# One-hot matrices of two tokens instead of four, built on a time budget, in a two-block transformer on one core

## The chip, the cores and the metric

The kernel runs on one NeuronCore of a Trainium2 chip. Its engines work side by side and wait for each other through semaphores: TensorE (PE, matmuls; PEld, its weight loads), VectorE (DVE), ScalarE (ACT), GpSimd (POOL) and SyncE (SP). Here SP only issues DMA transfers, and GpSimd only issues indirect ones. The metric is the device time of one execution in microseconds.

## What is computed

A sequence of 256 tokens with 1024 features passes two layers of a first block (four kinds of attention, then a gated MLP with a convolution) and two layers of a second block (a mixer, then a large mixture of experts). The change lies in the experts, `peer_ffn`. Each token has 8 heads, each head chooses 16 of 128 x 128 experts by the sum of two scores, and a softmax over the chosen scores gives the gates:

```python
    best_s, best_p = lax.top_k(cand_s, PEER_TOPK)
    idx = jnp.take_along_axis(cand_i, best_p, axis=-1)
    gate = jax.nn.softmax(best_s, axis=-1)
...
        act = jnp.einsum('td,thkd->thk', xb.astype(jnp.float32), u_tab[ib].astype(jnp.float32))
        wgt = jax.nn.gelu(act) * gb
        return jnp.einsum('thk,thkd->td', wgt, v_tab[ib].astype(jnp.float32))
```

## The kernel before

The kernel gathers no experts. In `peer` it multiplies all tokens with all 16384 rows of `u` (called U below), applies the gelu to the result, multiplies it with a dense table of gates that is zero where a token has not chosen an expert, and multiplies that with all of `v` (V). An expert has a number i * 128 + j; on chip i is the partition and j a column.

**Weights.** `weights` streams each matrix in units of 128 x 1024 fp32 (512 KB): SP issues the load into `wx` (3 buffers), ScalarE copies it to `wh` (4 buffers) with fewer mantissa bits, and VectorE writes the rest to `wl` (4 buffers, line 121). `mm3` then makes three matmuls for each product, with the high and low parts of the activations (`xh`, `xl`). U has 128 units in a layer, and so has V. `u_step` uses two units and fills two columns j of `at0` (j 0 to 63) or `at1` (j 64 to 127); 32 steps make a half of U.

**Gates.** The ranking (`select`) yields its work bit by bit, and `weave` puts it between the steps of U's first half: after each step, `beside` lets it have so many nanoseconds of VectorE by nominal costs, in the place behind the last `wl`. The gates of the two halves of the tokens then go two ways.
- The first 128 tokens: `scatter_gates` writes them into a zeroed table in HBM (`gates`) with 128 indirect DMAs of GpSimd (line 209), one for each head and rank. The 16 of a head wait until those of the head before have landed. `load_gates` (line 223) reads the table back on SP's queue, two columns j at a time, once the last head has landed; VectorE multiplies them into `at` (`v_split`), and `split` makes the high and low parts `eh` and `el` for V.
- The last 128 tokens: `build` makes the table's columns in PSUM. For four tokens it compares `io` with the chosen i and j (`oi`, `oj`), multiplies `oj` with three bf16 parts of the gates (`og`), and adds 12 matmuls of 128 x 128. VectorE multiplies the result into `at0` and into what `at1` holds so far; ScalarE copies the rest into `at1`, where later steps of U are multiplied in. One such group follows each step of U's second half.

**V.** `v_step` takes a pair of columns j (two units, 24 matmuls of 512 columns into the four banks `big`) and calls `v_split` for the next pair. The first pair is split by `first_split`, behind U.

The order of each engine's instructions is fixed when the program is built. The framework takes them from the code's order, lets an instruction go ahead of others where its own estimate of times says that it is ready, and inserts the semaphores. Each engine works its list in order, SP too.

Of the kernel before, what the change touches and what calls it, by code (L numbers as in the profile page):

```python
# [12 lines left out]
BF16 = mybir.dt.bfloat16  # L13
# [3 lines left out]
AF = mybir.ActivationFunctionType  # L17
OP = mybir.AluOpType
AX = mybir.AxisListType

T = 256
# [32 lines left out]
EARLY = 1  # L54
WARM = 10
LAG, TAIL, AHEAD, HOLD = 4, 2, 2, (2, 6)
SIDE_Q, SIDE_S = 2500, 2800
UQ_SIZES = [768, 512]
S2_SIZES = [1024] * 26

# [1 line left out]
class Net:  # L62
# [156 lines left out]

    def load_gates(self, l, n, pool):  # L220

        g = self.t(pool, [128, 2, 128], tag="gate", bufs=3)
        d = self.nc.sync.dma_start(g, self.gates[l][:, 2 * n:2 * n + 2]).ins
        for b in self.landed:
            self.tc.add_manual_dep(d, b.name, SYNC, reason="the gates have landed")
        return g
# [809 lines left out]
    def peer(self, l):  # L1036
# [3 lines left out]
        with ExitStack() as ctx:  # L1040
            ip = ctx.enter_context(self.pool("pi"))
            idx = self.t(ip, [128, 128], U32, tag="idx")
            gs = [self.t(ip, [128, 8, 16], tag=f"gs{tt}") for tt in range(2)]
            iT, jT = (self.t(ip, [128, 128], BF16, tag=n) for n in ("iT", "jT"))
            gT = self.t(ip, [128, 3, 128], BF16, tag="gT")
            io = self.t(ip, [128, 128, 4], BF16, tag="io")
            for _ in self.clear:
                pass
            self.clear = self.clear_gates(l + 1, 4) if l < DEPTH - 1 else iter(())
# [4 lines left out]
            def half_acts():  # L1054
                return self.t(ctx.enter_context(self.pool("pa")), [128, 64, T], tag="at")

            def u_step(at, jp, tb=0):

                ps = self.pj([128, 2, T])
                for m in range(2):  # L1060
                    self.proj_fm(w, ps[:, m])
                a = at[:, 2 * jp:2 * jp + 2]
                self.act(a[:, :, :T - tb], ps[:, :, :T - tb], AF.Gelu_apprx_tanh)
                if tb:
                    y = self.t(self.op, [128, 2, 128], tag="y", bufs=2)[:, :, :tb]
                    self.act(y, ps[:, :, T - tb:], AF.Gelu_apprx_tanh)
                    self.tt(a[:, :, T - tb:], a[:, :, T - tb:], y, OP.mult)

            def build(g):


                t0, done = 124 - 4 * g, 2 * g + 2
                oi, oj = (self.t(self.op, [128, 128, 4], BF16, tag=n, bufs=2) for n in ("oi", "oj"))
                og = self.t(self.op, [128, 3, 128, 4], BF16, tag="og", bufs=2)
                self.tt(oi, io, iT[:, None, t0:t0 + 4].to_broadcast([128, 128, 4]), OP.is_equal)
                self.tt(oj, io, jT[:, None, t0:t0 + 4].to_broadcast([128, 128, 4]), OP.is_equal)
                self.tt(og, oj[:, None].to_broadcast([128, 3, 128, 4]),
                        gT[:, :, None, t0:t0 + 4].to_broadcast([128, 3, 128, 4]), OP.mult)
                yield 1900
                ps = self.ps([128, 4, 128])  # L1080
                for k in range(4):
                    for n in range(3):
                        self.mm(ps[:, k], oi[:, :, k], og[:, n, :, k], k == 0 and n == 0, n == 2)
                ps = ps.rearrange("p t j -> p j t")
                t0 += 128
                a0, a1 = at0[:, :, t0:t0 + 4], at1[:, :, t0:t0 + 4]
                self.tt(a0, a0, ps[:, :64], OP.mult)
                self.tt(a1[:, :done], a1[:, :done], ps[:, 64:64 + done], OP.mult)
                if done < 64:
                    self.copy(a1[:, done:], ps[:, 64 + done:])  # L1090
                yield 700

            parts, loaded = {}, {}

            def g_load(n):
                if n < 64:
                    loaded[n] = self.load_gates(l, n, early)

            def v_split(n, pool):

                if n < 64:
                    g_load(n + 2)
                    a = (at0, at1)[n // 32][:, 2 * (n % 32):2 * (n % 32) + 2]
                    self.tt(a[:, :, :128], a[:, :, :128], loaded.pop(n), OP.mult)
                    h, low = (self.t(pool, [128, 2, T], F32R, tag=x, bufs=1 + (n > 0)) for x in ("eh", "el"))
                    self.split(h, low, a)
                    parts[n] = [(h[:, m], low[:, m]) for m in range(2)]

            def first_split():
                for n in range(2):  # L1110
                    g_load(n)
                v_split(0, early)

            def v_step(at, jp, half):
                units = [(next(w), x) for x in parts.pop(32 * half + jp)]
                last = half == 1 and jp == 31
                for u in [units] if last else [units[:1], units[1:]]:
                    self.out_tokens(u, half == 0 and jp == 0 and u[0] is units[0], last, end if last else None)
                    if u[0] is units[0]:
                        v_split(32 * half + jp + 1, vp)  # L1120
# [6 lines left out]
            def weave(step, side, per_step, then=None):  # L1127

                side = chain(side, (f() or 0 for f in [then] if f))
                left = 0.0  # L1130
                for jp in range(32):
                    step(jp)
                    left = self.beside(side, left + per_step)
                for _ in side:
                    pass
# [4 lines left out]
            with self.pool("pn") as npool:  # L1140
                lead = self.enter(npool, "add", self.v("n2"), w, self.t(npool, [128, 8, T], tag="xnew"))
                self.dump(f"xc{l}", self.xT)
                if l < DEPTH - 1:
                    nc.sync.dma_start(keep, self.xT)
                self.hctx.close()
                self.xctx.close()
                self.open_xs()
                pool = sctx.enter_context(self.pool("pk", "right"))
                self.token_column()
                if l == DEPTH - 1:  # L1150
                    nc.sync.dma_start(keep, self.rows_of(npool))
                it = self.t(pool, [128, 128], tag="iota")
                nc.sync.dma_start(it, self.a["iota"])
                io16 = self.t(pool, [128, 16, 128], BF16, tag="io16")
                rank = self.select(l, pool, w, lead, self.normed(npool, self.v("n2")), io16, gs, idx, (iT, jT, gT))
                self.copy(io16, it[:, 0:16, None].to_broadcast([128, 16, 128]))
                self.copy(io, it[:, :, None].to_broadcast([128, 128, 4]))
            self.xs = self.xh, self.xl
            at0 = half_acts()
            weave(lambda jp: u_step(at0, jp), rank, SIDE_S)  # L1160
            sctx.close()
            at1 = half_acts()
            with self.pool("po") as self.op:
                for g in range(32):
                    u_step(at1, g, 4 * g)
                    for _ in build(g):
                        pass
            early = ctx.enter_context(self.pool("pf"))
            first_split()
            self.hctx.close()  # L1170
            self.open_xt()
            if l < DEPTH - 1:
# [5 lines left out]
                end = to_output  # L1178
            vctx = ExitStack()
            vp = vctx.enter_context(self.pool("pv", "right"))  # L1180
            for half, at in enumerate((at0, at1)):
                weave(lambda jp: v_step(at, jp, half), iter(()), 0)
            vctx.close()
# [3 lines left out]
    def select(self, l, pool, w, lead, normed, io16, gs, idx, turned):  # L1187
# [63 lines left out]
        def rest_of_ranks():  # L1251
            yield from normed
            pend.sort(key=lambda x: x[0])
            for tt in range(2):
# [5 lines left out]
                for r in range(8):  # L1260
                    n = 16 if r == 0 else 8
                    o = 0 if r == 0 else 8 + 8 * r
# [5 lines left out]
                    yield 760  # L1268

                bt = best[tt]  # L1270
                g = gs[tt]
                self.tt(g, bt, bt[:, :, 0:1].to_broadcast([128, 8, 16]), OP.subtract)
                self.act(g, g, AF.Exp)
                s = self.t(pool, [128, 8], tag="s", bufs=2)
# [6 lines left out]
                pf = self.t(pool, [128, 128], tag="pf", bufs=2)  # L1281
# [19 lines left out]
                for c in range(2):  # L1301
                    f, e = (self.t(pool, [128, 16, 8, 16], BF16, tag=n) for n in ("fe", "e"))
                    self.copy(f, fa[:, :, c].rearrange("p h r -> p r h")[:, :, :, None].to_broadcast([128, 16, 8, 16]))
                    e, f = (x.rearrange("p r h k -> p r (h k)") for x in (e, f))
# [14 lines left out]
                iT, jT, gT = turned  # L1319
                ps = self.ps([128, 3, 128])  # L1320
# [8 lines left out]
                self.tt(gT[:, 2], rest, gT[:, 1], OP.subtract)  # L1329

        return rest_of_ranks()

    def run(self, parts=("f0", "f1", "s0", "s1")):
# [204 lines left out]
```

## Time and profile before

| | us |
|---|---|
| median of 3 runs | 2612.99 (2612.26 to 2613.42) |
| profiled execution | 2614.9 |
| its span | 2613.0 |
| TensorE busy | 2560.8 (98%) |
| VectorE busy | 1835.9 (70%) |
| ScalarE busy | 1383.7 (53%) |
| GpSimd busy | 463.4 (18%) |

The span runs from the first instruction to the last in the profiled execution; 1.9 us of the execution's time lie around it. Busy times of different engines overlap. The mean TensorE clock granted was 0.996 of full speed.

### The profile page before, as it was taken

To read this page: it belongs to the slowest core of one execution; us is meant where nothing else is said; L and a number is where in the kernel's file an instruction comes from. 1 tells how busy PE (TensorE), PEld (TensorE's weight loads), DVE (VectorE), ACT (ScalarE), POOL (GpSimd) and SP (SyncE) were. 2 spreads that over 40 slices of the span, in tenths; PEclk is the share of its full clock that TensorE was granted. 3 is DMA by queue.
4 is the path that set the end of the run, shared out by engine and by line. 5 is a ranking of instruction groups with operands and counts; after the bars stand their busy time and mean duration, and the time that the engine had idled before them with its cause. 6 is when DMAs were issued, how large, how long until landed. Compare 5 with 4: busy or idle time off the path is not lost.

```text
span 2613.0 us, 46153 instructions
## 1 busy us (share of the span) xinstructions
PE 2560.8 (98%) x18042; PEld 2366.2 (91%) x18042; DVE 1835.9 (70%) x3511; ACT 1383.7 (53%) x2128; POOL 463.4 (18%) x261
## 2 busy tenths in 40 slices
PE   8999999999999999999999999999999999999999
PEld 7799997999999999999878888999999999878887
DVE  6688777877887995666665555877994666675555
ACT  6565566655676554444444444776554443344443
POOL 0000000000000077773000000000178772000000
PEclk9999999999999999999999999999999999999999
DMA  8756652566535576665576666635576665676664
GB/s 281 235 179 192 183 174 79 153 192 183 175 116 185 170 185 186 149 150 149 193 249 203 194 194 193 185 107 187 173 191 179 148 150 148 212 248 194 194 194 158
DMA packets 195098, 470.95 MB, mean 180 GB/s; under 512 B 54644, under 2 KB 89588, under 8 KB 193856
## 3 DMA queue, kind: packets, MB, share of 16 engines
q1 hardware_dynamic: 158016, 467.86, 56.9%
q0 software_dynamic: 36864, 0.15, 3.6%
q8 instruction: 141, 2.31, 0.3%
q14 instruction: 77, 0.63, 0.1%
HBM read 447.86 MB, written 20.05 MB: 179 GB/s over the span
## 4 chain that ended last, share of the span: by engine, by line
PE 85%; DMA 6%; DVE 6%; ACT 2%; issue 1%; SPq 0%; ACTq 0%; DVEq 0%
PE pj L132 46%; PE big L132 31%; PE ps L132 7%; DMA gate<-gates 4%; DVE wl L121 2%; DMA wx<-in_w 1%; ACT wh L118 1%; PE ps L573 1%; DVE el L121 1%; DVE xn L124 0%; DVE at L121 0%; DVE xT L121 0%; DMA wx<-in_wq 0%; DVE xl L124 0%; DVE c L124 0%
## 5 line engine op out<-in xcount | busy, mean ns | idle before, releaser
L118 ACT ACTIVATE wh<-wx 128x1024 fp32r<-128x1024 f32 (+1 forms) x800 | 844.4, 1057 | 898.7 <-PE pj L132 356.1
L121 DVE TENSOR_TENSOR wl<-wx,wh 128x1024 fp32r<-128x1024 f32 (+1 forms) x800 | 975.0, 1220 | 453.8 <-ACT wh L118 446.4
L132 PE MATMUL pj<-xh,wh 128*128 128x256 f32 x3136 | 897.3, 286 | 10.5 <-ACT wh L118 7.9
L132 PE MATMUL pj<-xl,wh 128*128 128x256 f32 x3136 | 889.6, 284 | 3.3 <-DVE xl L124 2.7
L132 PE MATMUL pj<-xh,wl 128*128 128x256 f32 x3136 | 889.1, 284 | 3.8 <-DVE wl L121 3.8
L209 POOL DMA_INDIRECT gates<-gs,idx x256 | 462.9, 1808 | 1712.6 <-DVE idx L129 1591.8
L132 PEld LDWEIGHTS pj<-xh,wh 128*128 128x128 f32 x3136 | 601.2, 192 | 12.8 <-ACT wh L118 8.3
L132 PEld LDWEIGHTS pj<-xl,wh 128*128 128x128 f32 x3136 | 600.5, 191 | 7.9 <-DVE xl L124 6.5
L132 PEld LDWEIGHTS pj<-xh,wl 128*128 128x128 f32 x3136 | 599.9, 191 | 6.6 <-DVE wl L121 5.7
L132 PE MATMUL big<-wh,el 128*128 128x512 f32 x1024 | 402.1, 393 | 10.4 <-DVE el L121 10.3
L132 PE MATMUL big<-wh,eh 128*128 128x512 f32 x1024 | 400.0, 391 | 11.6 <-ACT eh L118 11.6
L132 PE MATMUL big<-wl,eh 128*128 128x512 f32 x1024 | 399.9, 390 | 0.0
L132 PEld LDWEIGHTS big<-wh,el 128*128 128x128 f32 x1024 | 193.1, 189 | 58.4 <-DVE el L121 19.2
L132 PEld LDWEIGHTS big<-wh,eh 128*128 128x128 f32 x1024 | 193.0, 189 | 52.6 <-ACT eh L118 12.2
L132 PEld LDWEIGHTS big<-wl,eh 128*128 128x128 f32 x1024 | 193.1, 189 | 39.6
L121 DVE TENSOR_TENSOR at<-at,ps 128x256 f32<-128x256 f32 (+20 forms) x128 | 45.1, 352 | 131.6 <-PE ps L132 131.6
L132 PE MATMUL ps<-og,oi 128*128 128x128 bf16 x768 | 101.5, 297 | 0.0
L132 PE MATMUL big<-gh,wh 128*128 128x256 f32 x352 | 99.1, 282 | 0.0
L132 PE MATMUL big<-gl,wh 128*128 128x256 f32 x352 | 98.9, 281 | 0.0
L132 PE MATMUL big<-gh,wl 128*128 128x256 f32 x352 | 98.8, 281 | 0.0
L121 DVE TENSOR_TENSOR at<-at,gate 128x256 f32<-128x256 f32 x128 | 52.9, 422 | 58.4 <-DMA gate<-gates 58.0
L121 DVE TENSOR_TENSOR el<-at,eh 128x512 fp32r<-128x512 f32 x128 | 87.2, 684 | 0.0
(355 smaller groups left out, 3309.0 us busy)
## 6 DMA issues: line engine op xcount, KB each, us to landing
wx<-in_u SPq DMA_DIRECT2D x256, 512.0 KB
wx<-in_v SPq DMA_DIRECT2D x256, 512.0 KB
wx<-in_wm SPq DMA_DIRECT2D x132, 512.0 KB
wx<-in_w SPq DMA_DIRECT2D x88, 512.0 KB
gates<-zero SPq DMA_DIRECT2D x128, 128.0 KB
wx<-in_wo SPq DMA_DIRECT2D x32, 512.0 KB
wx<-in_wq SPq DMA_DIRECT2D x32, 512.0 KB
gate<-gates SPq DMA_DIRECT2D x128, 128.0 KB
```

Source lines behind the costliest of these rows:

```text
L118: return self.nc.scalar.activation(out, in_, AF.Copy)
L121: return self.nc.vector.tensor_tensor(out, a, b, op=op)
L132: return self.nc.tensor.matmul(ps, w, x, start=start, stop=stop, skip_group_check=True)
L209: d = self.nc.gpsimd.indirect_dma_start(flat, IndirectOffsetOnAxis(ap=idx[:, p:p + 1], axis=0), g[:, p:p + 1], None, compute_op=OP.add).ins
L573: self.nc.tensor.transpose(tp[:, kt, qt * 128:(qt + 1) * 128], p[:, qt, kt * 128:(kt + 1) * 128], self.ident)
```

## The change

The one-hot matrices `oi` and `oj` now hold two tokens interleaved (innermost dimension 2) instead of four; a group still covers four tokens, as two parts, and `og` is made in two instructions of half the size. `build` becomes `builds`, a generator that `weave` runs beside the steps of U's second half on a budget of 3100 nominal ns for each step (a group counts 2750), with `first_split` behind the last group. The gate table for V's first pair gets a buffer of its own (`first`), which `load_gates` fills; the loads for pairs 1 and 2 are issued when V's pool is opened. The gelu of the columns whose gates are already there stays in PSUM (`y` is gone). `gs` has one buffer instead of two.

```diff
-SIDE_Q, SIDE_S = 2500, 2800
+SIDE_Q, SIDE_S, SIDE_G = 2500, 2800, 3100
...
-        g = self.t(pool, [128, 2, 128], tag="gate", bufs=3)
+        g = pool if n == 0 else self.t(pool, [128, 2, 128], tag="gate", bufs=3)
         d = self.nc.sync.dma_start(g, self.gates[l][:, 2 * n:2 * n + 2]).ins
         for b in self.landed:
             self.tc.add_manual_dep(d, b.name, SYNC, reason="the gates have landed")
...
-            io = self.t(ip, [128, 128, 4], BF16, tag="io")
+            io = self.t(ip, [128, 128, 2], BF16, tag="io")
+            first = self.t(ip, [128, 2, 128], tag="gate")
+            built = [0]
...
-                self.act(a[:, :, :T - tb], ps[:, :, :T - tb], AF.Gelu_apprx_tanh)
-                if tb:
-                    y = self.t(self.op, [128, 2, 128], tag="y", bufs=2)[:, :, :tb]
-                    self.act(y, ps[:, :, T - tb:], AF.Gelu_apprx_tanh)
-                    self.tt(a[:, :, T - tb:], a[:, :, T - tb:], y, OP.mult)
...
+                self.act(a[:, :, :n], ps[:, :, :n], AF.Gelu_apprx_tanh)
+                if built[0]:
+                    self.act(ps[:, :, n:], ps[:, :, n:], AF.Gelu_apprx_tanh)
+                    self.tt(a[:, :, n:], a[:, :, n:], ps[:, :, n:], OP.mult)
+
+            def builds(pairs):
+
+
+                for t0 in range(124, -1, -4):
+                    oi, oj = (self.t(self.op, [128, 2, 128, 2], BF16, tag=n, bufs=b) for n, b in (("oi", 2), ("oj", 1)))
+                    chosen = lambda x: x[:, t0:t0 + 4].rearrange("p (a t) -> p a t", t=2)[:, :, None].to_broadcast([128, 2, 128, 2])
+                    for o, x in ((oi, iT), (oj, jT)):
+                        self.tt(o, io[:, None].to_broadcast([128, 2, 128, 2]), chosen(x), OP.is_equal)
+                    ps = self.ps([128, 4, 128])
+                    for a in range(2):
+                        og = self.t(self.op, [128, 3, 128, 2], BF16, tag="og", bufs=3)
+                        self.tt(og, oj[:, a:a + 1].to_broadcast([128, 3, 128, 2]),
+                                gT[:, :, None, t0 + 2 * a:t0 + 2 * a + 2].to_broadcast([128, 3, 128, 2]), OP.mult)
...
+                    yield 2000
+                    ps, done = ps.rearrange("p t j -> p j t"), 2 * pairs[0]
...
+                    built[0] += 4
+                    yield 750
...
             def v_split(n, pool):
 
                 if n < 64:
-                    g_load(n + 2)
+                    if n:
+                        g_load(n + 2)
...
-            with self.pool("po") as self.op:
-                for g in range(32):
-                    u_step(at1, g, 4 * g)
-                    for _ in build(g):
-                        pass
-            early = ctx.enter_context(self.pool("pf"))
-            first_split()
+            early = ctx.enter_context(self.pool("pf"))
+            pairs = [0]
+
+            def u_second(jp):
+                u_step(at1, jp)
+                pairs[0] += 1
+
+            def first_split():
+                loaded[0] = self.load_gates(l, 0, first)
+                v_split(0, early)
+
+            with self.pool("po") as self.op:
+                weave(u_second, builds(pairs), SIDE_G, first_split)
...
+            for n in (1, 2):
+                g_load(n)
```

Where instructions stand now. On SP's queue, in U's first half of layer 0, these rows stood before (`wx_12649` is U's 51st load; in brackets the semaphores that an instruction waits for: DMAHW those of SP's transfers, DMASW those of GpSimd's indirect ones):

```order
L154 DMA wx_12619<-in_u 128x1024 [waits DMAHW5_49,DVE_49]
L154 DMA wx_12649<-in_u 128x1024 [waits DMAHW6_49,DVE_49]
L154 DMA wx_12681<-in_u 128x1024 [waits DMAHW7_49,DVE_49]
L154 DMA wx_12711<-in_u 128x1024 [waits DMAHW0_49,DVE_49]
L154 DMA wx_12744<-in_u 128x1024 [waits DMAHW1_49,DVE_49]
```

and these stand there now (`wx_12650` is the 51st load, `gate_9886` the buffer `first`):

```order
L154 DMA wx_12620<-in_u 128x1024 [waits DMAHW5_49,DVE_49]
L154 DMA wx_12650<-in_u 128x1024 [waits DMAHW6_49,DVE_49]
L223 DMA gate_9886<-gates_95 128x256 [waits DMASW4_49,DMASW5_49,DMASW3_49,DMASW6_49,DMASW2_49,DMASW7_49,DMASW1_49,DMASW0_49]
L154 DMA wx_12682<-in_u 128x1024 [waits DMAHW7_49,DVE_49]
L154 DMA wx_12712<-in_u 128x1024 [waits DMAHW0_49,DVE_49]
L154 DMA wx_12745<-in_u 128x1024 [waits DMAHW1_49,DVE_49]
```

The first gate load has moved from behind all 128 loads of U (and six of V) to a place between the 51st and the 52nd; in layer 1 it stands between the 51st and the 52nd as well. Where the first gate loads stood before, at the passage from U to V, SP's queue reads like this (`xT_15941` takes the place of U's activations):

```order
L154 DMA wx_16033<-in_v 128x1024 [waits DMAHW1_49,DVE_49]
L1173 DMA xT_15941<-keep_9889 128x2048 [waits PE_49]
L223 DMA gate_15926<-gates_95 128x256 [waits DMASW4_49,DMASW5_49,DMASW3_49,DMASW6_49,DMASW2_49,DMASW7_49,DMASW1_49,DMASW0_49]
L223 DMA gate_15928<-gates_95 128x256
L223 DMA gate_15930<-gates_95 128x256 [waits PE_49]
L154 DMA wx_16039<-in_v 128x1024 [waits DMAHW2_49,DVE_49]
```

The loads for pairs 1 and 2 are still behind `xT`; that for pair 0 is gone from here. On ScalarE, at the same passage, these rows stood before (`eh_15933` is the high part of V's first pair, the next two `eh` those of pairs 1 and 2; `wh_15869` and the four `wh` that follow it are V's first five units):

```order
L118 ACTIVATE wh_15954<-wx_15952 128x1024
L118 ACTIVATE wh_15991<-wx_15989 128x1024
L111 ACTIVATE at_13122<-pj_15835 128x2x132
L111 ACTIVATE y_15898<-pj_15835 128x2x124
L105 ACT_TABLE_LOAD
L118 ACTIVATE eh_15933<-at_10626 128x512
L118 ACTIVATE eh_15973<-at_10626 128x512
L118 ACTIVATE eh_16017<-at_10626 128x512
L118 ACTIVATE wh_15998<-wx_15995 128x1024
```

and these stand there now (`eh_16007` is pair 1, `eh_16051` pair 2, `wh_16032` and `wh_16069` V's fifth and sixth units):

```order
L111 ACTIVATE at_13123<-pj_15901 128x2x128
L111 ACTIVATE pj_15901<-pj_15901 128x2x128
L105 ACT_TABLE_LOAD
L118 ACTIVATE wh_16032<-wx_16029 128x1024
L118 ACTIVATE wh_16069<-wx_16067 128x1024
L118 ACTIVATE eh_16007<-at_10626 128x512
L118 ACTIVATE eh_16051<-at_10626 128x512
L118 ACTIVATE wh_16075<-wx_16073 128x1024
```

Pair 0's `eh` has moved up among U's last steps, and two `wh` of V now stand between U's last gelu and pair 1's `eh`.

## Rows read from the trace of the kernel before

**Rows 1.** The page: each engine's busy time, share of the span, instructions.

```profile
PE 2560.8 (98%) x18042; PEld 2366.2 (91%) x18042; DVE 1835.9 (70%) x3511; ACT 1383.7 (53%) x2128; POOL 463.4 (18%) x261
```

**Rows 2.** The chain that ended last, in time: start, us, what, matmuls.

```profile
862.38 126.00 PE pj L132 x1050
...
1373.81 265.28 PE big L132 x1169
...
1831.24 126.00 PE pj L132 x1050
```

**Rows 3.** Stretches: length, busy PE, PEld, DVE, ACT, POOL, granted clock, DMA, GB/s.

```profile
862.38:1051.90 189.52, 189.52 (x1582) 189.48 (x1581) 146.74 (x445) 98.49 (x113) 110.35 (x56) 1.00 0.67 181
1051.90:1276.00 224.10, 224.10 (x1874) 221.89 (x1872) 146.40 (x242) 92.62 (x157) 120.26 (x73) 1.00 0.59 147
1276.00:1290.00 14.00, 8.20 (x30) 6.57 (x30) 9.36 (x19) 5.09 (x7) 0.00 (x0) 0.76 0.71 244
1290.00:1373.00 83.00, 77.69 (x333) 61.44 (x332) 57.16 (x90) 35.59 (x41) 0.00 (x0) 1.00 0.80 251
```

**Rows 4.** GpSimd's timeline: start, us, instruction, idle time before it and its end.

```profile
914.05 1.65 POOL L209 DMA_INDIRECT gates<-gs,idx  x1 [913.00 <-DVE idx L129]
...
949.73 1.54 POOL L209 DMA_INDIRECT gates<-gs,idx  x1 [4.38 <-DMA gates<-gs,idx]
...
987.54 1.61 POOL L209 DMA_INDIRECT gates<-gs,idx  x1 [4.15 <-DMA gates<-gs,idx]
...
1001.34 2.57 POOL L209 DMA_INDIRECT gates<-gs,idx  x1 [0.30 <-issue]
...
1103.74 1.54 POOL L209 DMA_INDIRECT gates<-gs,idx  x1 [2.22 <-DMA gates<-gs,idx]
...
1202.51 1.54 POOL L209 DMA_INDIRECT gates<-gs,idx  x1 [0.30 <-issue]
...
2175.05 1.54 POOL L209 DMA_INDIRECT gates<-gs,idx  x1 [0.30 <-issue]
```

**Rows 5.** SP's timeline from U's first load on, two windows: start, us, loads.

```profile
843.69 147.28 SPq L154 DMA_DIRECT2D wx<-in_u  x51
...
843.69 151.15 SPq L154 DMA_DIRECT2D wx<-in_u  x52
```

**Rows 6.** The timeline at V's start in layer 0.

```profile
1274.52 0.33 SPq L1173 DMA_DIRECT2D xT<-keep  x1
1275.14 1.61 SPq L223 DMA_DIRECT2D gate<-gates  x3
...
1281.82 1.22 PE L132 MATMUL big<-wh,eh 128*128 128x512 f32 x2 [5.80 <-ACT eh L118]
...
1283.27 0.63 PE L132 MATMUL big<-wl,eh 128*128 128x512 f32 x1
...
1286.11 0.39 PE L132 MATMUL big<-wl,eh 128*128 128x512 f32 x1
```

**Rows 7.** VectorE's timeline beside the scatter.

```profile
1001.27 1.22 DVE L121 TENSOR_TENSOR wl<-wx,wh 128x1024 fp32r<-128x1024 f32 x1 [1.65 <-ACT wh L118]
```

**Rows 8.** The page's groups: `wh` on ScalarE; busy us, mean ns, idle before.

```profile
L118 ACT ACTIVATE wh<-wx 128x1024 fp32r<-128x1024 f32 (+1 forms) x800 | 844.4, 1057 | 898.7 <-PE pj L132 356.1
```

**Rows 9.** The chain that ended last, at its beginning.

```profile
1.66 5.15 DMA wx<-in_w
```

**Rows 10.** Build weight loads (timeline); instructions of tiles `oi`, `og`, `at` (ns min/median/max).

```profile
1152.40 1.29 PEld L132 LDWEIGHTS <-oi 128*128 128x128 bf16 x12
...
L121 DVE TENSOR_TENSOR oi<-io,iT x64: 410/418/466, 991.4 to 2232.6; 128x512 bf16<-128x512 bf16 x64
...
L121 DVE TENSOR_TENSOR og<-oj,gT x64: 943/950/954, 992.4 to 2233.0; 128x1536 bf16<-128x1536 bf16 x64
...
L121 DVE TENSOR_TENSOR at<-at,gate x128: 415/424/430, 1280.7 to 2342.8; 128x256 f32<-128x256 f32 x128
L118 ACT ACTIVATE eh<-at x128: 612/613/630, 1281.1 to 2598.8; 128x512 fp32r<-128x512 f32 x128
```

More of the change, by code (lines that the diff above doesn't have):

```diff
@@ L1042, in peer @@
             idx = self.t(ip, [128, 128], U32, tag="idx")
-            gs = [self.t(ip, [128, 8, 16], tag=f"gs{tt}") for tt in range(2)]
+            gs = self.t(ip, [128, 8, 16], tag="gs")
             iT, jT = (self.t(ip, [128, 128], BF16, tag=n) for n in ("iT", "jT"))
             gT = self.t(ip, [128, 3, 128], BF16, tag="gT")
-            io = self.t(ip, [128, 128, 4], BF16, tag="io")
+            io = self.t(ip, [128, 128, 2], BF16, tag="io")
+            first = self.t(ip, [128, 2, 128], tag="gate")
+            built = [0]
             for _ in self.clear:
@@ L1055, in half_acts, with u_step @@
                 return self.t(ctx.enter_context(self.pool("pa")), [128, 64, T], tag="at")
-            def u_step(at, jp, tb=0):
+            def u_step(at, jp):
                 ps = self.pj([128, 2, T])
@@ L1061, in u_step @@
                     self.proj_fm(w, ps[:, m])
-                a = at[:, 2 * jp:2 * jp + 2]
-                self.act(a[:, :, :T - tb], ps[:, :, :T - tb], AF.Gelu_apprx_tanh)
-                if tb:
-                    y = self.t(self.op, [128, 2, 128], tag="y", bufs=2)[:, :, :tb]
-                    self.act(y, ps[:, :, T - tb:], AF.Gelu_apprx_tanh)
-                    self.tt(a[:, :, T - tb:], a[:, :, T - tb:], y, OP.mult)
[L1069 to L1091, printed above, removed]
@@ new lines, in u_step @@
+                a, n = at[:, 2 * jp:2 * jp + 2], T - built[0]
+                self.act(a[:, :, :n], ps[:, :, :n], AF.Gelu_apprx_tanh)
[13 more added lines that the diff above has]
+                                gT[:, :, None, t0 + 2 * a:t0 + 2 * a + 2].to_broadcast([128, 3, 128, 2]), OP.mult)
+                        for k in range(2):
+                            for n in range(3):
+                                self.mm(ps[:, 2 * a + k], oi[:, a, :, k], og[:, n, :, k], a == 0 and k == 0 and n == 0,
+                                        n == 2)
+                    yield 2000
+                    ps, done = ps.rearrange("p t j -> p j t"), 2 * pairs[0]
+                    a0, a1 = (x[:, :, 128 + t0:132 + t0] for x in (at0, at1))
+                    self.tt(a0, a0, ps[:, :64], OP.mult)
+                    self.tt(a1[:, :done], a1[:, :done], ps[:, 64:64 + done], OP.mult)
+                    if done < 64:
+                        self.copy(a1[:, done:], ps[:, 64 + done:])
+                    built[0] += 4
+                    yield 750
@@ L1096, in g_load @@
                 if n < 64:
-                    loaded[n] = self.load_gates(l, n, early)
+                    loaded[n] = self.load_gates(l, n, vp)
             def v_split(n, pool):
                 if n < 64:
-                    g_load(n + 2)
+                    if n:
+                        g_load(n + 2)
                     a = (at0, at1)[n // 32][:, 2 * (n % 32):2 * (n % 32) + 2]
@@ L1107, in v_split @@
                     parts[n] = [(h[:, m], low[:, m]) for m in range(2)]
[L1109 to L1112, printed above, removed]
             def v_step(at, jp, half):
@@ L1156, in peer @@
                 self.copy(io16, it[:, 0:16, None].to_broadcast([128, 16, 128]))
-                self.copy(io, it[:, :, None].to_broadcast([128, 128, 4]))
+                self.copy(io, it[:, :, None].to_broadcast([128, 128, 2]))
             self.xs = self.xh, self.xl
@@ L1270, in rest_of_ranks @@
                 bt = best[tt]
-                g = gs[tt]
+                g = gs if tt == 0 else self.t(pool, [128, 8, 16], tag="g")
                 self.tt(g, bt, bt[:, :, 0:1].to_broadcast([128, 8, 16]), OP.subtract)
```

## The prediction

> **What bounds the kernel now.** I read the page first: TensorE is busy 98% of the span and every other engine has slack [rows 1], so time is lost or won only where TensorE stops. The chain of waits then gives the stage the change edits: in layer 0's expert stage TensorE starts U's first unit at 862.38, and 1050 of its matmuls take 126.00 us, which is 24 x 126.00 / 1050 = 2.88 us for a unit; in layer 1 the same piece begins at 1831.24 [rows 2]. The table by stage shows no idle TensorE in either half of U; behind U there are two short lossy stretches, 1276 to 1290 (8.20 busy of 14.00, granted clock 0.76) and 1290 to 1373 (77.69 of 83.00, DMA busy 0.80) [rows 3]. V's start is therefore worth at most 5.8 + 5.3 us of idle and some 2 us of clock in each layer.
>
> Next I read two queues that look idle or harmless. GpSimd scatters the first 128 tokens' gates into HBM with 128 indirect DMAs in a layer: the first starts at 914.05, when `idx` is ready, and the last at 1202.51 (layer 1: 2175.05) [rows 4]. Nobody waits for them before V. SP issues all weight loads in the order written: the 51st load of U leaves by 843.69 + 147.28 = 990.97, the 52nd by 994.84 [rows 5].
>
> **The change on SP: the term that decides.** The first gate load has moved from behind U to a place between the 51st and the 52nd load of U (the order rows above), and it carries the waits for all 8 semaphores of the scatter. At that place, 991, the scatter has 200 us to go. That a waiting load holds the one behind it on SP can be read at V's start: the first gate load there waits for nothing but the scatter, which had ended 70 us earlier, yet it leaves at 1275.14 only, just behind the load of `xT`, which waits for TensorE until 1274.52 (order rows) [rows 6]. So after 991 no weights are issued until the scatter has landed. TensorE has 51 units and works until 862.38 + 51 x 2.88 = 1009.3.
>
> *When the scatter lands.* It goes in eight groups (heads) of 16, each waiting for the landing of the one before; the third starts at 987.54 [rows 4]. An undisturbed operation takes 1.54 us with 0.30 before it, pitch 1.85 [rows 4]. Around 1001 it takes 2.57: the one at 1001.34 starts just behind a `wl` of VectorE at 1001.27 (1.22 long), and the 1.03 us added is about what is left of that `wl` [rows 4, 7]. In the stall VectorE has nothing, so I take 1.85 from 1001.34 on, where six of the third head's sixteen are done: 10 x 1.85 - 0.30 gives 1019.5. Between heads the landing takes 2.22 (the least of layer 0's seven gaps) to 4.38 (the most) [rows 4]; I take 2.7, near the quiet end, since the weight traffic has stopped. Five more heads of 2.7 + 15 x 1.85 + 1.54 = 32.0 and a last landing: 1019.5 + 160.0 + 2.7 = 1182.2. Bounds: all gaps 2.22 gives 1179.3, all 4.38 gives 1192.3.
>
> [...]
>
> *Until TensorE runs again.* 0.5 us for SP to issue the gate load and the 52nd unit; 5.2 from issue to landing, as for the program's first weight load (5.15 from 1.66 on [rows 9], with other transfers around it; here a gate load goes ahead and two units follow); 1.06 for `wh`, 1.22 for `wl` [rows 7, 8], which the third matmul needs: 1190.2. TensorE has then idled 180 us. After 5.80 us idle it ran at half clock for a while: a 128x512 matmul shows 0.63, later 0.39 [rows 6]. So I give unit 52's other 22 matmuls 0.24 instead of 0.12: 1195.5, where before the unit ends at 862.38 + 52 x 2.88 = 1012.1. **Shift: 183.4 us in a layer** (181 if the clock returns at once). Behind it loads, splits and U keep their old pace, so nothing is regained.
>
> **The change at V's start.** Before, TensorE idles 5.80 us for pair 0's `eh` and starts V at 1281.82 [rows 6]. Afterwards V's first pair (24 matmuls of 265.28 / 1169 = 0.227 us [rows 2], 5.45 in all) is split during U and runs at once when U ends (E). Pair 1 still waits: ahead of its `eh` on ScalarE stands `wh` of V's sixth unit (order rows), which needs the buffer that the second unit of pair 0 gives back at E + 5.45; then 1.06 for it, 1.22 for its `wl`, which stands before pair 1's gate product on VectorE, 0.42 for the product and 0.61 for `eh` [rows 10]: E + 8.8. The idle moves there and shrinks from 5.80 to 3.4. With less time at half clock I take a gain of 3 us (bounds: 0, if the DMA-bound stretch to 1373 (busy 0.80 [rows 3]) takes it back; 8, if the whole pair and the clock are kept).
>
> **What I cost at nothing.** `og` in two parts: 768 elements lie between `oi` (512 elements, 418 ns) and the old `og` (1536, 950 ns) [rows 10]; on the line between them 0.55, so 1.10 for 0.95, +4.9 us of VectorE in a layer (from -3.6 to +30). It hides in U's second half, where VectorE is busy 146.40 of 224.10 [rows 3]; uncovered it would cost those 4.9. 32 groups of 2750 on a budget of 3100 a step end in step 29 of 32; before, one stood in each step, so TensorE does the same 384 short matmuls, only earlier. The gelu that now stays in PSUM and the one buffer less of `oj` keep a `pj` or `oj` longer, but each is freed over a step (5.75 us) before it is wanted.
>
> *Interleaving two one-hots.* Twelve weight loads from `oi` take 1.29 us, 107.5 ns each [rows 10]; that sets the short matmuls' pace. No row here shows a load with a stride of two, so: unchanged at the one end, the half at the other, 768 x 0.054 = 41 us less. I take unchanged: the tokens of a one-hot stay non-adjacent.
>
> [...]
>
> **The sum.** 183.4 - 3 = 180.4 in each layer, 360.8 in two. The layers agree: in layer 1 the last scatter starts 343.8 us behind U's start, in layer 0 340.1. The profiled execution took 2614.9 (span 2613.0 and 1.9 around it): 2975.7. The median of the runs is 1.9 lower, so **2974 us**, 13.8% slower.
>
> **Rivals.**
> - *The scatter keeps its old times* (landing 1202.51 + 1.54 + 2.7 = 1206.8): for it, later heads ran beside VectorE with nearly undisturbed operations, so less may be won; against it, the slow ones stand where `wl` runs. 24.6 more in a layer: 3023. Chance 0.06.
> - *The slow pace isn't VectorE's doing* but belongs to a quiet machine (it came when VectorE had least to do). Then 90 operations take 1.03 more: 3159. Against it: the step beside each `wl`. Chance 0.03.
> - *The short matmuls halve:* 2933. Chance 0.06.
> - *The other side: the gate load holds nobody.* If its wait were kept elsewhere than in SP's queue, or the scatter landed before unit 52 is due (by about 1002, 7 us ahead of 1009.3), only V's start would change: 2613 - 2 x 3 = 2607. Against it: the gate load that stood behind `xT` with nothing to wait for, and 200 us between 1002 and the scatter's end. Chance 0.05.
> - The forecast itself: 0.80, on its own between 2952 and 3000 (landing 1179 to 1192, V's start 0 to 8).
>
> **Numbers.** The range runs from 2933 (halved matmuls) to 3023 (old scatter times); outside lie 3159 and 2607, 0.08, and little of the middle case. Within 0.2% is about what a measurement of this kernel can tell from no change. Slower 0.95; faster 0.03 and same 0.02 share the other side's chance, as its gain of 0 to 16 us straddles 5 us.
>
> **What the profile should show.** One wait of some 190 us on SP before line 223 in each layer, ended by an indirect DMA; TensorE idle some 180 us between U's 51st and 52nd units, and its busy share near 86% with unchanged busy time; GpSimd's operations at 1.54 from about 1001 on; three quick weight loads behind the scatter's end; unit pitch 2.88 again after some microseconds of half clock; short matmuls still 107 ns apart; no idle before V's first pair and some 3 us behind it. I am wrong if the 52nd load leaves before the scatter lands; mis-sized if heads take other than 32 us in the stall.

## The result, and the profile after

| | before | after |
|---|---|---|
| median | 2613.2 us (2612.26 to 2613.85, 4 runs) | 2924.35 us (2921.17 to 2926.86, 4 runs) |
| profiled execution's span | 2613.0 us | 2921.2 us |
| mean granted clock | 0.996 | 0.937 |

The changed kernel is 11.9% slower: ratio 1.1194, 95% interval 1.1181 to 1.1208. The forecast was 2974 (2933 to 3023). The kernel is slower, and by the stall that the forecast named, but the time is 50 us below the forecast and 9 below the range: the forecast took a gain of 42 us in the short matmuls at nothing.

The page of the changed kernel: TensorE's busy time, then its busy tenths and the granted clock in 40 slices of the span.

```profile
PE 2518.2 (86%) x18042; PEld 2325.1 (80%) x18042; DVE 1836.1 (63%) x3575; ACT 1389.4 (48%) x2130; POOL 414.5 (14%) x261
...
PE   8999999999999700899999999999910499999999
...
PEclk9999999999999855899999999999955699999999
```

Two things differ from [rows 1]. The span has two holes, one in each layer, in which TensorE does nothing and the granted clock is down at half (0.50 from 1002 to 1180). And TensorE's busy time, with the same 18042 matmuls, went from 2560.8 to 2518.2: 42.6 us that the forecast didn't have. GpSimd's fell too, from 463.4 to 414.5.

TensorE's waits: line, what released it, us in total, times, the longest.

```profile
PE pj L132 <- ACT at L111: 357.6, 2, 179.1
...
PE big L132 <- ACT eh L118: 6.4, 2, 3.2
```

SP's waits name the cause: in each layer line 223, the first gate load, waits for the scatter's transfers (on four of its semaphores, 188.2 us in layer 0 and 187.7 in layer 1).

```profile
SPq L223 <- DMA gates<-gs,idx: 375.9, 8, 182.8
```

SP's timeline in layer 0 has nothing else from 986.51 (980.42 + 6.09) to 1174.93, 188 us. Before, the 52nd load had left by 994.84 [rows 5].

```profile
980.42 6.09 SPq L154 DMA_DIRECT2D wx<-in_u  x3
1174.93 0.33 SPq L223 DMA_DIRECT2D gate<-gates  x1
1175.35 24.18 SPq L154 DMA_DIRECT2D wx<-in_u  x11
```

VectorE's timeline on both sides of the last `wl` before the stall, and GpSimd's there (in brackets the idle time before, and what ended it):

```profile
984.93 1.23 DVE L121 TENSOR_TENSOR wl<-wx,wh 128x1024 fp32r<-128x1024 f32 x1 [1.66 <-ACT wh L118]
...
993.94 1.23 DVE L121 TENSOR_TENSOR wl<-wx,wh 128x1024 fp32r<-128x1024 f32 x1 [1.66 <-ACT wh L118]
```

```profile
985.00 2.58 POOL L209 DMA_INDIRECT gates<-gs,idx  x1 [0.30 <-issue]
...
994.01 2.58 POOL L209 DMA_INDIRECT gates<-gs,idx  x1 [0.30 <-issue]
996.89 1.55 POOL L209 DMA_INDIRECT gates<-gs,idx  x1 [0.30 <-issue]
...
1017.39 1.54 POOL L209 DMA_INDIRECT gates<-gs,idx  x1 [2.29 <-DMA gates<-gs,idx]
...
1048.92 1.54 POOL L209 DMA_INDIRECT gates<-gs,idx  x1 [2.19 <-DMA gates<-gs,idx]
...
1171.83 1.54 POOL L209 DMA_INDIRECT gates<-gs,idx  x1 [0.30 <-issue]
```

An operation that starts just behind a `wl` takes 2.58; from the end of the last `wl` on, all take 1.55. With weights and VectorE quiet, a head takes 31.5 us (1048.92 - 1017.39).

The timeline of all engines where the stall of layer 0 ends, loads left out:

```profile
1179.04 1.06 ACT L118 ACTIVATE wh<-wx 128x1024 fp32r<-128x1024 f32 x1 [185.14 <-DMA wx<-in_u]
1180.01 0.58 ACT L111 ACTIVATE at<-pj 128x512 f32<-128x512 f32 x1
1180.13 1.23 DVE L121 TENSOR_TENSOR wl<-wx,wh 128x1024 fp32r<-128x1024 f32 x1 [184.97 <-ACT wh L118]
...
1180.64 0.58 PE L132 MATMUL pj<-xh,wh 128*128 128x256 f32 x1 [179.12 <-ACT at L111]
...
1181.02 0.41 PE L132 MATMUL pj<-xl,wh 128*128 128x256 f32 x1
...
1181.23 0.41 PE L132 MATMUL pj<-xh,wl 128*128 128x256 f32 x1
...
1184.43 0.28 PE L132 MATMUL pj<-xh,wl 128*128 128x256 f32 x1
```

Read it from the top: weights land, ScalarE makes `wh` of unit 52, and only then runs the gelu (`at<-pj`) that TensorE waits for. That gelu's matmuls (units 47 and 48; units 51 and 52 need their `pj` again, of which there are two) were done some 184 us earlier; it stands behind `wh` on ScalarE. Then the matmuls come 0.21 apart until 1184.43 (granted clock 0.50) and 0.12 apart behind it (1.00). In layer 1 the slow ones last longer, 27 matmuls from 2305.06 to 2310.91:

```profile
2305.06 0.58 PE L132 MATMUL pj<-xh,wh 128*128 128x256 f32 x1 [178.43 <-ACT at L111]
...
2310.91 0.28 PE L132 MATMUL pj<-xh,wh 128*128 128x256 f32 x1
```

The chain that ended last: start, us, what, matmuls. Its first row here lies in the part of the program that both kernels share.

```profile
118.80 17.38 PE big L132 x145
...
857.93 36.60 PE pj L132 x305
...
1230.14 5.80 PE pj L132 x48
1235.93 0.70 PE ps L132 x12
1236.64 5.80 PE pj L132 x48
...
1983.04 36.60 PE pj L132 x305
```

And the matmuls of tile `oi` on TensorE (ns min/median/max), in which that gain lies, after and before, with a group of them in the chain before:

```profile
L132 PE MATMUL ps<-og,oi x768: 217/218/231, 1228.5 to 2533.2; 128*128 128x128 bf16 x192
```

```profile
L132 PE MATMUL ps<-og,oi x768: 281/297/302, 1051.9 to 2244.6; 128*128 128x128 bf16 x192
```

```profile
1138.20 1.43 PE ps L132 x12
```

Twelve short matmuls now take 0.70 us in the chain, 58 ns each; before they took 1.43, and their loads stood 107.5 ns apart [rows 10]. (A matmul's own duration, 218 ns in the median for 58 from one to the next, overlaps with the next one's.)

V's start in layer 0 (timeline):

```profile
1431.00 0.40 PE L132 MATMUL big<-wh,eh 128*128 128x512 f32 x1
...
1436.44 1.06 ACT L118 ACTIVATE wh<-wx 128x1024 fp32r<-128x1024 f32 x1 [1.26 <-DVE wl L121]
1437.53 1.23 DVE L121 TENSOR_TENSOR wl<-wx,wh 128x1024 fp32r<-128x1024 f32 x1 [1.09 <-ACT wh L118]
...
1439.12 1.15 ACT L118 ACTIVATE eh<-at 128x512 fp32r<-128x512 f32 x2 [1.63 <-DVE at L121]
...
1439.81 1.58 PE L132 MATMUL big<-wh,eh 128*128 128x512 f32 x4 [3.18 <-ACT eh L118]
```

Pair 0 runs without a wait; 3.18 us of idle stand in front of pair 1, where 5.80 stood in front of pair 0 [rows 6].

### The profile page after: what moved, and what is told of

Its sections match the earlier page's. It is cut to its first block, busy times and chain, and to the rows that moved or that the text cites. A ratio compares the mean times of both kernels' runs of the same rounds, so it can differ in the third digit from the quotient of the medians.

```text
span 2921.2 us, 46151 instructions
## 1 busy us (share of the span) xinstructions
PE 2518.2 (86%) x18042; PEld 2325.1 (80%) x18042; DVE 1836.1 (63%) x3575; ACT 1389.4 (48%) x2130; POOL 414.5 (14%) x261
## 4 chain that ended last, share of the span: by engine, by line
PE 69%; POOL 13%; DMA 6%; DVE 5%; issue 4%; ACT 2%; POOLq 0%; SPq 0%; ACTq 0%; DVEq 0%
PE pj L132 35%; PE big L132 28%; POOL gates L209 13%; PE ps L132 5%; DMA gate<-gates 3%; DMA gates<-gs,idx 2%; DVE wl L121 2%; ACT wh L118 1%; PE ps L573 1%; DVE el L121 1%; DVE xn L124 0%; DMA wx<-in_w 0%; DVE xT L121 0%; DVE at L121 0%; DVE xl L124 0%
## 5 line engine op out<-in xcount | busy, mean ns | idle before, releaser
L132 PE MATMUL pj<-xh,wh 128*128 128x256 f32 x3136 | 898.8, 287 | 368.1 <-ACT at L111 357.6
L209 POOL DMA_INDIRECT gates<-gs,idx x256 | 414.0, 1617 | 1882.9 <-DVE idx L129 1770.1
L118 ACT ACTIVATE eh<-at 128x512 fp32r<-128x512 f32 x128 | 78.4, 614 | 3.3 <-DVE at L121 3.3
L124 DVE SCALAR_TENSOR_TENSOR c<-lz,v,c 128x255 f32<-128x255 f32 x176 | 73.8, 478 | 0.8 <-ACT c L111 0.6
```

The source lines that it names most:

```text
L118: return self.nc.scalar.activation(out, in_, AF.Copy)
L124: return self.nc.vector.scalar_tensor_tensor(out, a, s, b, op0=op0, op1=op1)
L132: return self.nc.tensor.matmul(ps, w, x, start=start, stop=stop, skip_group_check=True)
L209: d = self.nc.gpsimd.indirect_dma_start(flat, IndirectOffsetOnAxis(ap=idx[:, p:p + 1], axis=0), g[:, p:p + 1], None, compute_op=OP.add).ins
```

## The experiments

The chips of these runs gave 2614 to 2615 us (medians) for the kernel before. Times are medians, ratios are to the kernel before with a 95% interval.

**1. Is it the queue?** (on the changed kernel) The first gate load keeps its place in the program and its wait for the scatter, but is issued from GpSimd, which issues the scatter itself.

```diff
-        d = self.nc.sync.dma_start(g, self.gates[l][:, 2 * n:2 * n + 2]).ins
+        d = (self.nc.gpsimd if n == 0 else self.nc.sync).dma_start(g, self.gates[l][:, 2 * n:2 * n + 2]).ins
```

> The changed kernel with one edit: the load of V's first gates is issued by GpSimd, behind its own scatter, and no longer by SP. Theory (the wait on SP holds the weights): both stalls of 179 us vanish; what is left of the change is the quicker short matmuls (2 x 21.7 us) and V's start (2 x 2 us), so about 2565 us. Rival (the early product and split, or the new order of the groups, cost the time): it stays above 2900 us. Second rival (the 4.7 us that the changed kernel's trace is ahead before layer 0's experts belong to the change): 2560.

Measured: 2564.82 us, 0.9806 (0.9785 to 0.9826). TensorE's longest waits in this kernel:

```profile
PE big L132 <- DVE el L121: 11.3, 17, 1.2
...
PE big L132 <- ACT eh L118: 6.4, 2, 3.2
```

The 179 us waits are gone, and all 360 us with them. On GpSimd's queue, which has nothing else to do here, the wait for the scatter costs nothing: TensorE's longest single wait is 8.0 us there, and was 7.9 in the kernel before.

**2. Or its place on SP?** (on the changed kernel) The load stays on SP, and also waits for a late split, so that it stands near the end of U's loads.

```diff
+        if n == 0:
+            self.tc.add_manual_dep(d, self.low.ins.name, SYNC, reason="behind a late split")
```

> The changed kernel with one more dependency: the load of V's first gates stays on SP but also waits for the last low part of the weights written when it is asked for, so that the scheduler puts it behind the 125th load of U. Theory: the scatter has landed by then, SP holds nobody, about 2565 us, as with the load on GpSimd. Rival (a gate load before U's end costs weights in any place): above 2600 us.

Measured: 2563.96 us, 0.9804 (0.9787 to 0.9821). SP's timeline has it at 1226.85, between U's loads:

```profile
961.37 263.21 SPq L154 DMA_DIRECT2D wx<-in_u  x84
1226.85 0.33 SPq L223 DMA_DIRECT2D gate<-gates  x1
1227.28 6.66 SPq L154 DMA_DIRECT2D wx<-in_u  x3
```

Same engine, same buffer, same data: only the place in the queue differs from the changed kernel, and 360 us with it. This version and that of run 1 beat both kernels.

**3. The gate load alone** (on the kernel before): `first` has a buffer of its own and is loaded early; one-hots stay as they were, the build too (but `oj` has one buffer), and V's first pair is split where it was. SP has the load between U's 51st and 52nd again.

```diff
-        g = self.t(pool, [128, 2, 128], tag="gate", bufs=3)
+        g = pool if n == 0 else self.t(pool, [128, 2, 128], tag="gate", bufs=3)
...
+            first = self.t(ip, [128, 2, 128], tag="gate")
...
-                for n in range(2):
-                    g_load(n)
+                g_load(1)
...
+            loaded[0] = self.load_gates(l, 0, first)
```

> The kernel before with the other part of the change alone: the load of V's first gates is asked for ahead of U's second half into a buffer of its own (and oj has one buffer instead of two, for space); groups, their four interleaved tokens and the split stay. The scheduler puts the load between U's 51st and 52nd units, as in the changed kernel. Theory (the wait is the whole loss): two stalls of 179 us and 1.6 us each of half clock, 2613 + 361 = about 2974 us. Rival (the loss needs the new order of the groups): near 2613.

Measured: 2967.61 us, 1.1346 (1.1323 to 1.1369).

```profile
PE pj L132 <- ACT at L111: 356.4, 2, 178.4
```

By itself this edit costs 354 us (2967.6 - 2614.0). The 6 us that it stays below the expected 2974 fit V's start, where TensorE's wait for `eh` is 3.3 us in all and was 11.6 in the kernel before. It is slower than the whole change by 43 us: the rest of the change is a gain.

**4. Does the scatter's end set the stall?** (on the changed kernel) Heads 4 to 7 aren't scattered, so half of the first tokens' gates are missing in the output, and the load waits for half as many operations. It stands behind U's 38th load there.

```diff
-        for h in range(8):
+        for h in range(4):
```

> The changed kernel with half of the scatter left out (four of eight heads, so the first 128 tokens lose half of their gates). The scheduler then puts the gate load behind the 38th load of U. Theory (the stall lasts until the last scattered head has landed): TensorE stops about 107 us behind U's start and goes on at about 192, idle 85 instead of 179 us in each layer, 2924 - 2 x 94 = about 2736 us. Rival (the stall has another end than the scatter's): idle near 179 + 13 x 2.88 = 216 us, about 3000 us.

Measured: 2734.31 us (one run).

TensorE's longest wait, and from the chain the row that answers to the first one of the changed kernel's:

```profile
PE pj L132 <- ACT at L111: 161.4, 2, 81.0
```

```profile
125.24 17.37 PE big L132 x145
```

GpSimd's last operation in layer 0, and SP's gate load behind it:

```profile
1042.25 1.55 POOL L209 DMA_INDIRECT gates<-gs,idx  x1 [0.30 <-issue]
```

```profile
1045.32 0.33 SPq L223 DMA_DIRECT2D gate<-gates  x1
```

The idle falls from 357.6 to 161.4 us, by 196. The program's beginning, which has no edit, took 6.4 us longer in this execution (125.24 for 118.80), so the time fell by 190. The gate load leaves 1.5 us behind the last operation's end, as in the changed kernel (1.6): the stall ends with the scatter.

**5. The one-hots alone** (on the kernel before): `oi`, `oj` and `og` interleaved by two, nothing moved. This is the part of the diff that the forecast took at nothing.

```diff
+                oi = self.t(self.op, [128, 2, 128, 2], BF16, tag="oi", bufs=2)
...
+                og = self.t(self.op, [128, 2, 3, 128, 2], BF16, tag="og", bufs=2)
...
-                        self.mm(ps[:, k], oi[:, :, k], og[:, n, :, k], k == 0 and n == 0, n == 2)
+                        self.mm(ps[:, k], oi[:, k // 2, :, k % 2], og[:, k // 2, n, :, k % 2], k == 0 and n == 0, n == 2)
```

> The kernel before with one part of the change: one-hots of two tokens interleaved instead of four (oi, oj, og), nothing moved. Theory (the distance between a one-hot's elements sets the pace of the short matmuls): 0.68 us less in each of 64 groups, so 2613 - 43.5 = about 2570 us, twelve weight loads in 0.69 us. Rival (the short matmuls are quicker because of where they stand in the changed kernel): 2613 us, 1.29.

Measured: 2572.86 us, 0.9839 (0.9821 to 0.9857), 42 us less than before on its chip.

**6. The weights' distance or the moving operand's?** (on the kernel before) One run has only the weights `oi` by two, the other only `oj` and the moving operand `og`.

```diff
-                        self.mm(ps[:, k], oi[:, :, k], og[:, n, :, k], k == 0 and n == 0, n == 2)
+                        self.mm(ps[:, k], oi[:, k // 2, :, k % 2], og[:, n, :, k], k == 0 and n == 0, n == 2)
```

> The kernel before with only the stationary one-hot (oi, loaded as weights) interleaved by two; the moving operand og stays interleaved by four. Theory (the weight load's distance of 8 bytes between elements sets the pace): 59 ns for a short matmul, about 2571 us. Rival (the moving operand's distance sets it): 107 ns, 2614 us. Third (both do): between, or 107 ns.

```diff
-                        self.mm(ps[:, k], oi[:, :, k], og[:, n, :, k], k == 0 and n == 0, n == 2)
+                        self.mm(ps[:, k], oi[:, :, k], og[:, k // 2, n, :, k % 2], k == 0 and n == 0, n == 2)
```

> The mirror of the run before: only oj and og interleaved by two, oi by four. Theory (weights set the pace): 107 ns, 2614 us. Rival (the moving operand sets it): 59 ns, 2571 us.

Measured: weights by two 2613.91 us, 0.9995 (0.9985 to 1.0006); moving operand by two 2574.67 us, 0.9842 (0.9816 to 0.9869). The chain in both, weights by two first:

```profile
1136.60 5.75 PE pj L132 x48
1142.36 1.41 PE ps L132 x12
1143.76 5.75 PE pj L132 x48
```

```profile
1133.20 5.80 PE pj L132 x48
1139.00 0.74 PE ps L132 x12
1139.73 5.80 PE pj L132 x48
```

and the loads' timeline in the second:

```profile
1158.46 0.73 PEld L132 LDWEIGHTS <-oi 128*128 128x128 bf16 x12
```

The weights' distance changes nothing, against the theory that the loads set the pace. The moving operand's gives nearly all of it: with the same weights, still 8 bytes from one element to the next, a load takes 0.73 / 12 = 61 ns. The 107.5 was the pace of the matmuls with the old `og`, for which the loads waited.

**7. Is two close enough?** (on the kernel before) No interleaving: each token's one-hot is contiguous, and `og` is made by three products.

```diff
-                        self.mm(ps[:, k], oi[:, :, k], og[:, n, :, k], k == 0 and n == 0, n == 2)
+                        self.mm(ps[:, k], oi[:, k], og[:, n, k], k == 0 and n == 0, n == 2)
```

> The kernel before with no interleaving: each token's one-hot is contiguous in oi, oj and og. Theory (59 ns is the pace of 128 columns, and two interleaved already reach it): short matmuls at 59 ns or little less (down to 54), 2570 us or up to 4 us less; VectorE's products, whose second operand then repeats its innermost element, get slower (og 512 elements each, three of them), hidden in U if all of it stays under 7 us a step. Rival (the quicker loads at two are a part of a longer slope): well under 50 ns, 2560 us or less. Second rival (VectorE becomes the bound): TensorE waits for og in U's second half, above 2590 us.

Measured: 2571.27 us, 0.9829 (0.9804 to 0.9855), not told apart from run 5 (each against the kernel before on its chip). A piece of its chain, and the making of `oi` on VectorE (ns min/median/max):

```profile
1138.41 0.69 PE ps L132 x12
```

```profile
L121 DVE TENSOR_TENSOR oi<-io,iT x64: 678/685/730, 986.8 to 2187.4; 128x512 bf16<-128x512 bf16 x64
```

Contiguous operands give 0.69 for 0.70: two tokens interleaved already reach the pace of contiguous ones. VectorE pays for them, 685 ns for 418, hidden here.

## Where the prediction was right, and where it failed

**The account.** From U's start to U's start of the next layer it took 1831.24 - 862.38 = 968.86 us before [rows 2] and 1983.04 - 857.93 = 1125.11 after, 156.25 more; from there to the end of the span 781.76 and 938.16, 156.40 more. U began 862.38 - 857.93 = 4.45 us earlier, in a part where both kernels do the same; executions differ there (run 4 by 6.4). 156.25 + 156.40 - 4.45 = 308.2, the difference of the spans. The forecast was 180.4 a layer.

**The stall (forecast 183.4 a layer): right, 180.9 and 181.0.** TensorE idles 179.12 us in layer 0 and 178.43 in layer 1. Its slow matmuls add 1.75 in layer 0 (the 17 that start from 1180.64 to before 1184.43 take 3.79 us, and 17 x 0.12 would be 2.04) and 2.61 in layer 1 (27 take 5.85, and 27 x 0.12 would be 3.24). Runs 1 and 2 remove it through the queue alone, run 3 makes it alone, run 4 halves it. Step by step:

- *The scatter's landing.* Forecast 319.8 us behind U's start (1182.2 - 862.38), measured 317.0 at most, for the gate load leaves at 1174.93. The last five heads took 158.3 us (from 996.89 + 9 x 1.85 + 1.55 = 1015.1 to 1171.83 + 1.54) for a forecast of 160.0, as their gaps were shorter than the 2.7 I took, and the last landing 1.6 for 2.7. That VectorE's `wl` had made operations slow is borne out to the operation: 2.58 behind a `wl`, 1.55 from the last one's end on. With that the two rivals on slower operations (3023, 3159) fall.
- *The restart.* 13.3 us from the landing to the end of unit 52 in the forecast (1195.5 - 1182.2) and in the trace (1180.64, two units of 2.88 and 1.75 make 1188.15; 1188.15 - 1174.9 = 13.25). That is partly luck: ScalarE had the weights 3.7 us behind their issue (1175.35 to 1179.04), not 5.2, and the clock cost 1.75, not 2.6 (in layer 1 it cost the 2.6); but TensorE had stopped one unit early, at 1180.64 - 179.12 = 1001.5, so unit 51 had still to be done. I had TensorE working off all units whose weights had come; I overlooked that ScalarE, too, works in order, and that the gelu which frees unit 51's `pj` stands behind the `wh` of unit 52 (`wh` at 1179.04, the gelu at 1180.01).

**The interleaving (forecast: unchanged): this step failed.** It read: twelve weight loads from `oi` take 107.5 ns each, and "that sets the short matmuls' pace". The row was right and its reading wrong: loads and matmuls alternate, and a row of loads that keep a pace doesn't say which of the two keeps it. Runs 5 to 7 settle it. A step of two units and a group takes 6.50 us (1236.64 - 1230.14) where it takes 7.16 with the old `og` (run 6, weights by two: 1143.76 - 1136.60); 0.66 x 64 = 42 us. The forecast with these 42 us in it would have been 2932; with 2.5 and 2.4 less for the stalls of the two layers, 2927. The rival that had this size, 2933 at a chance of 0.06, was put on the weights' stride; its mechanism falls as well, and run 6 shows the other.

The half at the other end of that step, 41 us less, was an estimate of mine. No run shows loads that halve by their own stride: with the weights by two, twelve short matmuls take 1.41 us and the program 2613.91 (run 6). What the runs show in its place is 42 us by the moving operand: once that is close, the same loads, at 8 bytes' distance, come 61 ns apart where they stood 107.5 apart (run 6, moving operand by two).

**V's start (forecast 3 a layer): right.** The idle went from 5.80 to 3.18 (forecast 3.4), by the chain that was forecast: `wh` at 1436.44, just behind E + 5.45 (E is 1431.00), `wl` until 1438.76, `eh`, TensorE at 1439.81, E + 8.8. From V's first matmul to layer 1's U it took 549.42 before and 552.04 after, 2.62 more, against 5.80 saved ahead of it: 3.2 won. Runs 1 and 2 beside run 5 give 8.0 and 8.9 in two layers; TensorE's wait for `eh` there is 13.6 us in all in run 5 and 6.4 and 6.3 in runs 1 and 2. The stretch behind it that the forecast called DMA-bound (DMA busy 0.80 before [rows 3]) took nothing back.

**What was costed at nothing.** `og` in two parts takes 553 ns each (forecast 0.55) and hides, as the build on its budget does: in the chain steps of 5.80 and groups of 0.70 (in a few places two groups, 1.51) follow each other with nothing between. From U's start to V's first matmul layer 0 took 1281.82 - 862.38 = 419.44 us before [rows 2, 6] and 1431.00 - 857.93 = 573.07 after, 153.6 more; the terms make 180.9 - 32 x 0.66 - 5.8 = 154.0, so nothing of that size is left over.

**The other side (2607 if the gate load holds nobody, chance 0.05).** What it asked for, a wait kept out of SP's queue, is run 1; there the time is 2565, not 2607, again by the 42 us of the interleaving.

## What to carry to other kernels

An early load on an in-order DMA queue is only as early as its last wait (here SP's queue stood still for 188 us in each layer): look for what is queued behind it and when that is due, and issue it from the queue of the engine that produces its data, or give it a dependency that puts it behind the loads due earlier. Where two kinds of instructions alternate, the duration or pace of one doesn't say which sets it (here 107.5 ns a load became 61 with the same weights); look at the other's operands too, here the moving operand's inner distance, worth 42 us. When a stall is priced, follow every in-order engine (ScalarE here) to find where the waiting engine really stops.

## What the hardware showed that was not expected

- The moving operand's distance: twelve matmuls of 128 bf16 columns take 1.41 us when a row's elements lie 8 bytes apart (run 6, weights by two), and 0.70 and 0.69 at 4 and 2 bytes (the changed kernel and run 7): at 8 bytes they run at half the pace of 4, and from 4 to 2 next to nothing is won.
- The weights' distance hardly counts here: 61 ns a load at 8 bytes (moving operand by two), 58 at 4 (the changed kernel).
- After 179 and 178 us without a matmul TensorE ran at half clock (granted 0.50 and 0.51) for 3.79 us in layer 0 and 5.85 in layer 1, and at full clock (1.00) from there on; in run 3, too, matmuls stand 0.21 apart behind the stall (1180.85 to 1181.92). Before, after 5.80 us of idle, half clock showed 1.45 us behind the restart and full clock 4.29 behind it [rows 6] (granted 0.50 until 1283.27, 1.00 from 1286.11 on). By these numbers thirty times the idle added at most some 5 us of half clock.
- The shared beginning of the program took from 118.80 to 125.24 us (123.62 in the kernel before) in executions of kernels that don't differ there; differences of a few us between spans are to be read from a place behind it.
